# A narrow projection as four 32-column fp32 blocks side by side, and history transposes moved into the head, in a hybrid SSD and pooling decoder step

## The chip, the core and the metric

The kernel runs on one core of one Trainium2 chip. The metric is the device time of one execution in microseconds. Engines are named as in the profile: PE is TensorE's matrix work and PEld its weight loads, DVE is VectorE, ACT is ScalarE, POOL is GpSimd, SP is the engine that issues most DMAs.

## The reference

`x` is 1024 prompt tokens and 64 sample tokens (8 sequences of 8) of width 1024, in fp32. The part that the change touches:

```
h    = rmsnorm(x) * norm_pre                       # 1088 tokens x 1024
proj = h @ w_in                                    # split into z | xBC (1536) | dt (16) | u | g | gates (2048)
xBC  = silu(causal_conv4(concat(state_conv, xBC))) # sample rows start from 3 history rows per sequence
dt   = softplus(proj_dt + dt_bias)                 # 16 columns, one for each head
y    = ssd_scan(xBC, dt, -exp(a_log))              # everything of branch A waits for dt
```

Behind it come the gate by z and the grouped norm, a pooling branch, the two branch projections, the sigmoid merge, the output projection with a norm, and the states.

## The kernel before

Activations are held transposed, with model channels on the 128 partitions: `h` is split into two tiles `Hhi` and `Hlo` (128 x 8 blocks of channels x 1088 tokens) whose sum is the fp32 value; both are stored in a reduced form (fp32r) that PE streams in one pass. A projection takes three products for each of the 8 channel blocks (hi by hi, lo by hi, hi by lo), in three chunks of tokens (384, 384, 320), so a chunk is a group of 24 matmuls into one bank (`psum_main`, two banks with the tag `m0`). Weights come by DMA in slabs of 128 columns and are split the same way: ACT casts `whi`, then POOL or DVE subtracts for `wlo` (`split`, L94 and L95).

The order of everything is written out by hand. The list `main` holds PE's groups, one for each slot; `at(slot, fn, key)` puts work of the other engines behind a slot's group, sorted by key, and `at_pe` puts PE work ahead of it. Each engine then works its own list strictly in that order. The slots that matter here:

- slots 0 to 5: two conv tiles (`cv[0]`, `cv[1]`), chunk by chunk; slots 6 to 8: the three chunks of `cv[8]`; slot 9: the dt projection (`DtStep.group`); then `cv[10]` and so on.
- For a conv group of slot t, ACT copies the bank out in slot t+1 (`evac`, L335) and makes the first tap (L343), DVE does three taps in slot t+2 (`taps`, L349), and in slot t+3 ACT takes a tanh (L356) of their result and DVE combines it (`fin`, L357, L360).
- The head, before slot 0 and in the first slots, is the string `plan`: N is a squared sum of a tile of 128 tokens, S and D scale it (DVE, L210), T and U transpose its two halves (PE, L224), E and F split them into `Hhi` and `Hlo`, W splits a weight slab, H is a filler matmul of the identity by itself (L1156) whose result nobody reads.
- The dt step: `load` brings the 16 columns, `conv` splits them into 32 of 128 columns of `dsw` (hi beside lo, the rest zero), `group` runs 16 matmuls for each chunk, `evac` copies 32 rows, `tok` (L416) transposes them to tokens, `softplus` adds the two partial sums and goes on.
- `hist_T` transposes the 24 rows of conv history at slot 5 (L291), twice six transposes, and DVE copies them out.

Of the kernel before, what the change touches and what calls it, by code (L numbers as in the profile page):

```python
# [38 lines left out]
def hybrid_decoder_step(  # L39
# [47 lines left out]
    def bank(tag):  # L87
        return px.tile([128, 512], F32, tag=tag, name=nm(tag))
# [16 lines left out]
    def at_pe(slot, fn, *args, first=False):  # L105
        pe[slot].insert(0 if first else len(pe[slot]), (fn, args))
# [161 lines left out]
        nc.sync.dma_start(prow[68:72], pool_scale[0].rearrange("(t p) -> t p", p=128))  # L268

    def hist_dma():  # L270
        for hf in range(2):
            hr = pbox["h", hf] = s1.tile([24, 768], F32, tag="xn", bufs=4, name=nm("xn"))
            nc.sync.dma_start(hr, state_conv[0].rearrange("b k c -> (b k) c")[:, 768 * hf:768 * hf + 768])
        for q in range(2):
            nc.sync.dma_start(dsk[64 * q:64 * q + 64],
                              d_skip[0].rearrange("(j q) -> q j", q=2)[q].partition_broadcast(64),
                              allow_slow_non_contiguous=True)
        nc.sync.dma_start(bias_b, dt_bias[0].partition_broadcast(128))
        nc.sync.dma_start(na, a_log[0].partition_broadcast(128))

    def params_T():
# [2 lines left out]
        nc.vector.tensor_scalar(par[:, 0:60], ps[:, 0:60], 0.5, None, op0=ALU.mult)  # L284
        nc.vector.tensor_copy(par[:, 60:72], ps[:, 60:72])

    def hist_T():
        for hf in range(2):
            ps = bank("pst")
            for i in range(6):  # L290
                nc.tensor.transpose(ps[:, 24 * i:24 * i + 24], pbox["h", hf][:, 128 * i:128 * i + 128], ident[0:24, 0:24])  # L291
            nc.vector.tensor_copy(histc[hf], ps[:, 0:144].rearrange("p (i k) -> p i k", i=6))
        nc.scalar.activation(na, na, AF.Exp)
        nc.vector.tensor_scalar(na, na, -1.0, None, op0=ALU.mult)

# [73 lines left out]

    class DtStep:  # L370
        def load(self):
            self.raw = s1.tile([128, 8, 16], F32, tag="dst", name="dst")
            nc.sync.dma_start(self.raw, w_in[0].rearrange("(k p) e -> p k e", p=128)[:, :, C_DT:C_DT + 16])
            self.w = s1.tile([128, 8, 128], F32R, tag="dsw", name="dsw")
            nc.gpsimd.memset(self.w.bitcast(F32), 0.0)

        def conv(self):
            split(self.w[:, :, 0:16], self.w[:, :, 16:32], self.raw, nc.gpsimd)

        def group(self):  # L380
            box = {}

            def emit():
                for c, (a, b) in enumerate(CHUNKS):
                    ps = box[c] = bank(("m0", "pyo", "pyo")[c])
                    for k in range(8):
                        for p, h in enumerate((Hhi, Hlo)):
                            nc.tensor.matmul(ps[:, 0:b - a], self.w[:, k], h[:, k, a:b], start=k == 0 and p == 0,  # L388
                                             stop=k == 7 and p == 1)

            main.append(emit)
            t = len(main) - 1
# [12 lines left out]
        def evac(self, box):  # L405
            self.dtr = zt((32, LT))
            self.tmp = zt((128, 5, 9, 16))
            nc.gpsimd.memset(self.tmp[64:128, 0, 8], 0.0)
            for c, (a, b) in enumerate(CHUNKS):
                nc.scalar.copy(self.dtr[:, a:b], box[c][0:32, 0:b - a])  # L410

        def tok(self):
            self.pd = bank("pst")
            for t in range(9):
                n = 128 if t < 8 else NS
                nc.tensor.transpose(self.pd[0:n, 32 * t:32 * t + 32], self.dtr[:, 128 * t:128 * t + n], ident[0:32, 0:32])  # L416
            zfree(self.dtr)

        def softplus(self):
            v, tt, u, e, r = (self.tmp[:, i] for i in range(5))  # L420
            self.adt = v
            for n, t0, m in ((128, 0, 8), (NS, 8, 1)):
                d = v[0:n, t0:t0 + m]
                nc.vector.tensor_reduce(d, self.pd[0:n, 32 * t0:32 * t0 + 32 * m].rearrange("p (t i h) -> p t h i", t=m, i=2),
                                        axis=mybir.AxisListType.X, op=ALU.add)
# [722 lines left out]
    nrow = hst[0:1].rearrange("p u x -> p (u x)")  # L1148
    nc.sync.dma_start(nrow, norm_pre)
    loads = {"W": lambda i: cv[i].slab.dma(raw1[:, 0:1024].rearrange("p (k e) -> p k e", k=8) if i else None),  # L1150
             "X": load_x, "Q": lambda i: params_dma()}
    for w in "X0 X1 X2 X3 W0 Q0 X4 W1 X5 X6 X7 X8".split():
        loads[w[0]](int(w[1]))

    def H(i):
# [2 lines left out]
    def R(e):  # L1158
# [351 lines left out]
```

## Time and profile before

| | |
|---|---|
| median of 3 runs | 894.23 us (893.12 to 894.34) |
| the profiled execution | 894.35 us, span 892.6 us |
| PE busy | 879.9 us of the span (99%) |
| DVE, ACT, POOL busy | 62%, 39%, 24% |
| mean granted TensorE clock | 0.997 of 2.4 GHz |

PE is busy nearly all the time, so what moves the time is what lengthens or shortens PE's own list and what makes PE wait. A row of the chronological view has a start, a length, engine, line, operation, output and inputs, shapes, the count of merged instructions and, in brackets, how long the engine stood idle before and what ended that. Lengths of successive matmuls overlap; the distance between two starts is what one costs.

### The profile page before, as it was taken

The page shows a single profiled execution, that of the slowest core. Times are in us where ns is not written, and L with a number is a line of the kernel's source. Part 1 is how long each engine was busy: PE and PEld are TensorE (multiplying, and loading weights), DVE is VectorE, ACT ScalarE, POOL GpSimd, SP SyncE. Part 2 cuts the span into 40 slices and gives each one's busy share as a digit, 9 for nine tenths or more (in the row PEclk, how much of TensorE's full clock was granted, in tenths as well). Part 3 has the DMA queues.
Part 4 walks back from the last instruction along what each step waited for, and adds up shares of the span by engine and source line. Part 5 has one row for each costly group of instructions (what it writes and reads, how often), then busy time and mean ns, then how long its engine had stood idle before and what let it go on. Part 6 is the DMA issues. An engine that isn't in the chain of part 4 may idle for free.

```text
span 892.6 us, 14398 instructions
## 1 busy us (share of the span) xinstructions
PE 879.9 (99%) x5558; PEld 843.7 (95%) x5558; DVE 551.2 (62%) x999; ACT 348.8 (39%) x770; POOL 217.4 (24%) x297
## 2 busy tenths in 40 slices
PE   7999999999999999999999999999999999999997
PEld 5999999999999999999999999999999999988886
DVE  6776796989667765457746554357356627963322
ACT  6645565656375543345333141112333224331111
POOL 6332264756465652121100000000000000001101
PEclk9999999999999999999999999999999999999999
DMA  8010233342345335453311124433111123722322
GB/s 275 9 48 24 77 95 97 99 128 71 103 129 156 105 96 164 127 160 101 95 49 36 54 84 149 143 114 99 34 49 51 31 79 115 264 74 71 100 99 85
DMA packets 110322, 87.97 MB, mean 99 GB/s; under 512 B 8474, under 2 KB 97550, under 8 KB 110253
## 3 DMA queue, kind: packets, MB, share of 16 engines
q1 hardware_dynamic: 110109, 86.98, 32.5%
q8 instruction: 44, 0.72, 0.3%
q14 instruction: 25, 0.20, 0.1%
q10 hardware_dynamic: 144, 0.07, 0.0%
HBM read 69.46 MB, written 17.56 MB: 97 GB/s over the span
## 4 chain that ended last, share of the span: by engine, by line
PE 93%; DVE 1%; ACT 1%; POOL 1%; issue 0%; DVEq 0%; POOLq 0%; ACTq 0%
PE m L143 54%; PE pyo L143 16%; PE m L1399 3%; PE pyo L1399 3%; PE xb L1399 2%; PE pst L1399 2%; PE pyo L575 2%; PE pyo L582 2%; PE pst L586 1%; PE xb L711 1%; PE xb L542 1%; PE pyo L388 1%; DVE r L841 1%; PE pyo L752 1%; PE pst L759 0%
## 5 line engine op out<-in xcount | busy, mean ns | idle before, releaser
L143 PE MATMUL m<-Hhi,whi 128*128 128x384 f32 (+3 forms) x872 | 289.0, 331 | 0.0
L143 PE MATMUL m<-Hhi,wlo 128*128 128x384 f32 (+3 forms) x872 | 285.4, 327 | 0.0
L143 PE MATMUL m<-Hlo,whi 128*128 128x384 f32 (+3 forms) x872 | 285.3, 327 | 0.0
L143 PEld LDWEIGHTS m<-Hhi,whi 128*128 128x128 f32 x872 | 164.6, 189 | 0.6
L143 PEld LDWEIGHTS m<-Hlo,whi 128*128 128x128 f32 x872 | 164.6, 189 | 0.3
L143 PEld LDWEIGHTS m<-Hhi,wlo 128*128 128x128 f32 x872 | 164.4, 189 | 0.3
L349 DVE SCALAR_TENSOR_TENSOR r<-r,par,r 128x384 f32<-128x384 f32 (+3 forms) x108 | 94.6, 876 | 2.6
L94 ACT CAST whi<-raw 128x1024 fp32r<-128x1024 f32 (+1 forms) x67 | 59.8, 892 | 91.4 <-PE m L143 53.6
L95 DVE TENSOR_TENSOR wlo<-raw,whi 128x512 fp32r<-128x512 f32 (+1 forms) x46 | 43.4, 944 | 65.2 <-ACT whi L94 65.1
L95 POOL TENSOR_TENSOR wlo<-raw,whi 128x1024 fp32r<-128x1024 f32 x21 | 51.6, 2457 | 40.9 <-ACT whi L94 40.9
L143 PE MATMUL pyo<-Hhi,whi 128*128 128x384 f32 (+1 forms) x184 | 59.8, 325 | 0.0
L143 PE MATMUL pyo<-Hhi,wlo 128*128 128x384 f32 (+1 forms) x184 | 59.7, 325 | 0.0
L143 PE MATMUL pyo<-Hlo,whi 128*128 128x384 f32 (+1 forms) x184 | 59.7, 324 | 0.0
L143 PE MATMUL m<-z,whi 128*128 128x384 f32 (+1 forms) x217 | 54.0, 327 | 0.0
L143 PE MATMUL pyo<-z,whi 128*128 128x384 f32 (+1 forms) x191 | 47.7, 327 | 0.0
L568 POOL TENSOR_TENSOR sa<-sa,cb 128x512 f32<-128x512 f32 x28 | 39.8, 1441 | 3.7 <-ACT sa L564 3.7
L143 PEld LDWEIGHTS m<-z,whi 128*128 128x128 f32 x217 | 38.4, 188 | 0.0
L143 PE MATMUL m<-z,wlo 128*128 128x384 f32 (+1 forms) x115 | 37.6, 327 | 0.0
L563 ACT ACTIVATE sa<-sa,acm 128x128 f32<-128x128 f32 x112 | 35.6, 389 | 0.0
L609 DVE SCALAR_TENSOR_TENSOR z<-z,dsk,se 128x128 f32<-128x128 f32 x56 | 34.8, 660 | 1.0
L1434 POOL TENSOR_SCALAR t<-t 128x1 f32<-128x1 f32 (+1 forms) x9 | 2.5, 276 | 133.7 <-ACT q L1431 133.7
L143 PEld LDWEIGHTS pyo<-Hlo,whi 128*128 128x128 f32 x184 | 34.6, 188 | 0.0
(386 smaller groups left out, 1608.5 us busy)
## 6 DMA issues: line engine op xcount, KB each, us to landing
raw<-in_w_in_dram SPq DMA_DIRECT2D x43, 512.0 KB, 4.0
z<-in_x_prompt_dram SPq DMA_DIRECT2D x15, 512.0 KB, 4.5
sa<-dscr SPq DMA_DIRECT2D x28, 256.0 KB, 4.4
z<-spill SPq DMA_DIRECT2D x11, 544.0 KB, 5.1
raw<-in_w_branch_a_dram SPq DMA_DIRECT2D x16, 256.0 KB, 2.8
r<-in_w_out_dram SPq DMA_DIRECT2D x16, 256.0 KB, 4.4
se<-dscr SPq DMA_DIRECT2D x56, 64.0 KB, 3.8
out_dram<-q SPq DMA_DIRECT2D x14, 256.0 KB, 2.1
```

Of the source, the lines that this page charges most:

```text
L94: nc.scalar.copy(hi, src)
L95: (eng or nc.vector).tensor_tensor(lo, src, hi.bitcast(F32), op=ALU.subtract)
L143: nc.tensor.matmul(ps[:, 0:b - a], slab.w(k, p), rhs(k, p)[:, a:b], start=k == 0 and p == 0, stop=k == slab.kn - 1 and p == 2)
L349: nc.vector.scalar_tensor_tensor(A, R[:, k:k + w], cw(k, i), A, op0=ALU.mult, op1=ALU.add)
L388: nc.tensor.matmul(ps[:, 0:b - a], self.w[:, k], h[:, k, a:b], start=k == 0 and p == 0, stop=k == 7 and p == 1)
L542: nc.tensor.transpose(p[:, 128 * i:128 * i + 128], X[2 * self.u + i][:, self.cols], ident)
L563: nc.scalar.activation(A[:, h], A[:, h], AF.Relu, bias=acm[:, self.c, hh:hh + 1], scale=-1.0)
L568: nc.gpsimd.tensor_tensor(A, A, CBs[self.c, self.g].unsqueeze(1).to_broadcast([128, 4, 128]), op=ALU.mult)
L575: nc.tensor.matmul(py[64 * q:64 * q + 64, 128 * i:128 * i + 128], s.x0[:, 2 * i + q], s.A[:, 2 * i + q], start=True, stop=True)
L582: nc.tensor.matmul(py[:, 256 + 128 * i:384 + 128 * i], hs[:, 128 * i:128 * i + 128], Ct[self.g][:, self.cols], start=True, stop=True)
L609: nc.vector.scalar_tensor_tensor(xv, xv, dsk[:, j:j + 1], self.E[:, i] if self.c else py[:, 128 * i:128 * i + 128], op0=ALU.mult, op1=ALU.add)
L1399: nc.tensor.matmul(box["ps"][:, 0:b - a], lh, rh[k][:, a:b], start=kk == 0 and i == 0, stop=kk == 7 and rh is Wlo)
```

## The change

The dt weights stay whole fp32, in 32 columns of which 16 are filled (the rest zero); nothing is split. DVE makes eight fp32 tiles `h[k] = Hhi[k] + Hlo[k]` (`whole`, 128 x 1088 each), two behind each of slots 5 to 8. In slot 9 each chunk takes 8 fp32 matmuls of 32 output columns: four of them go to the four 32-column parts of the array and to four 32-partition parts of the bank, each with another channel block, and a second round of four adds to them. The four partial sums are transposed along (full 128 x 128 transposes, now in two `xb` banks and one `pst` bank) and added up in DVE's reduce.

The 24 history rows are loaded in three pieces early in SP's list, ahead of x tile 4; their twelve transposes (`I0`) stand in the head, in one `m0` bank, and ACT copies them out (`J0`) instead of DVE. Six more fillers H stand in the head.

```diff
     def hist_dma():
-        for hf in range(2):
-            hr = pbox["h", hf] = s1.tile([24, 768], F32, tag="xn", bufs=4, name=nm("xn"))
-            nc.sync.dma_start(hr, state_conv[0].rearrange("b k c -> (b k) c")[:, 768 * hf:768 * hf + 768])
...
+    def hist_load():
+        for i in range(3):
+            pbox["h", i] = rt(512)[0:24]
+            nc.sync.dma_start(pbox["h", i], state_conv[0].rearrange("b k c -> (b k) c")[:, 512 * i:512 * i + 512])
+
     def hist_T():
+        ps = pbox["hp"] = bank("m0")
+        for i in range(12):
+            nc.tensor.transpose(ps[:, 24 * i:24 * i + 24], pbox["h", i // 4][:, 128 * (i % 4):128 * (i % 4) + 128], ident[0:24, 0:24])
+
+    def hist_copy():
         for hf in range(2):
-            ps = bank("pst")
-            for i in range(6):
-                nc.tensor.transpose(ps[:, 24 * i:24 * i + 24], pbox["h", hf][:, 128 * i:128 * i + 128], ident[0:24, 0:24])
-            nc.vector.tensor_copy(histc[hf], ps[:, 0:144].rearrange("p (i k) -> p i k", i=6))
+            nc.scalar.copy(histc[hf], pbox["hp"][:, 144 * hf:144 * hf + 144].rearrange("p (i k) -> p i k", i=6))
...
     class DtStep:
         def load(self):
-            self.raw = s1.tile([128, 8, 16], F32, tag="dst", name="dst")
-            nc.sync.dma_start(self.raw, w_in[0].rearrange("(k p) e -> p k e", p=128)[:, :, C_DT:C_DT + 16])
-            self.w = s1.tile([128, 8, 128], F32R, tag="dsw", name="dsw")
-            nc.gpsimd.memset(self.w.bitcast(F32), 0.0)
-
-        def conv(self):
-            split(self.w[:, :, 0:16], self.w[:, :, 16:32], self.raw, nc.gpsimd)
+            self.w = s1.tile([128, 8, 32], F32, tag="dsw", name="dsw")
+            nc.gpsimd.memset(self.w, 0.0)
+            nc.sync.dma_start(self.w[:, :, 0:16], w_in[0].rearrange("(k p) e -> p k e", p=128)[:, :, C_DT:C_DT + 16])
+
+        def whole(self, k):
+            if k == 0:
+                self.h = []
+            self.h.append(zt())
+            nc.vector.tensor_tensor(self.h[k], Hhi[:, k].bitcast(F32), Hlo[:, k].bitcast(F32), op=ALU.add)
...
                 for c, (a, b) in enumerate(CHUNKS):
                     ps = box[c] = bank(("m0", "pyo", "pyo")[c])
-                    for k in range(8):
-                        for p, h in enumerate((Hhi, Hlo)):
-                            nc.tensor.matmul(ps[:, 0:b - a], self.w[:, k], h[:, k, a:b], start=k == 0 and p == 0,
-                                             stop=k == 7 and p == 1)
+                    for r in range(2):
+                        for g in range(4):
+                            k = 4 * r + g
+                            nc.tensor.matmul(ps[32 * g:32 * g + 32, 0:b - a], self.w[:, k], self.h[k][:, a:b], start=r == 0,
+                                             stop=r == 1, tile_position=(0, 32 * g))
+                zfree(*self.h)
...
-    for w in "X0 X1 X2 X3 W0 Q0 X4 W1 X5 X6 X7 X8".split():
+    for w in "X0 X1 X2 X3 W0 Q0 Y0 X4 W1 X5 X6 X7 X8".split():
...
-    plan = ("R0 N0 R1 H0 N1 D0 H0 T0 U0 S1 N2 H0 S2 T1 N3 U2 T2 F0 W0 S3 E0 U1 E1 H0 T3 H0 U3 N4 F1 D4 W1 | "
+    plan = ("R0 N0 R1 H0 N1 D0 H0 T0 U0 S1 N2 H0 S2 T1 N3 H0 H0 U2 T2 F0 W0 S3 E0 U1 E1 I0 H0 H0 H0 H0 T3 J0 H0 U3 N4 F1 D4 W1 | "
...
-    at_pe(5, hist_T)
+    at(4, na_T, key=9)
...
-    at(6, dts.conv, key=5)
+    for k in range(8):
+        at(5 + k // 2, dts.whole, k, key=9)
```

On DVE, the stretch that ends with slot 9 stood so before (r are the conv's work tiles, z its outputs; L349 are the taps, L357 and L360 the combinations with the tanh):

```order
L357 SCALAR_TENSOR_TENSOR z_349<-r_694,r_607 128x384
L360 SCALAR_TENSOR_TENSOR z_349<-r_694,r_607 128x64
L349 SCALAR_TENSOR_TENSOR r_647<-r_640,par,r_647 128x472 x3
L357 SCALAR_TENSOR_TENSOR z_390<-r_731,r_647 128x384
L360 SCALAR_TENSOR_TENSOR z_390<-r_731,r_647 128x64
L349 SCALAR_TENSOR_TENSOR r_692<-r_689,par,r_692 128x384 x3
L357 SCALAR_TENSOR_TENSOR z_688<-r_798,r_692 128x384
L349 SCALAR_TENSOR_TENSOR r_729<-r_726,par,r_729 128x384 x3
```

and stands so in the changed kernel, where L363 and L366 are the combinations, L355 the taps and L386 the new sums:

```order
L363 SCALAR_TENSOR_TENSOR z_380<-r_710,r_617 128x384
L366 SCALAR_TENSOR_TENSOR z_380<-r_710,r_617 128x64
L355 SCALAR_TENSOR_TENSOR r_661<-r_654,par,r_661 128x472 x3
L386 TENSOR_TENSOR z_717<-Hhi,Hlo 128x1088
L386 TENSOR_TENSOR z_719<-Hhi,Hlo 128x1088
L363 SCALAR_TENSOR_TENSOR z_421<-r_751,r_661 128x384
L366 SCALAR_TENSOR_TENSOR z_421<-r_751,r_661 128x64
L355 SCALAR_TENSOR_TENSOR r_708<-r_705,par,r_708 128x384 x3
L386 TENSOR_TENSOR z_758<-Hhi,Hlo 128x1088
L386 TENSOR_TENSOR z_760<-Hhi,Hlo 128x1088
L363 SCALAR_TENSOR_TENSOR z_704<-r_798,r_708 128x384
L355 SCALAR_TENSOR_TENSOR r_749<-r_746,par,r_749 128x384 x3
```

The last pair of sums (channel blocks 6 and 7) stands behind the taps of slot 8, which are those of `cv[8]`'s first chunk; two pairs like these stand earlier, behind the taps of slots 5 and 6.

On ACT in the head, before (xn are normalised token tiles, raw and z_120 weight slabs; L201 is the squared sum of x tile 4, L94 the casts):

```order
L94 CAST Hhi<-pyo_192 128x4x128
L201 ACTIVATE xn_245,t_243<-z_137 128x1024
L94 CAST Hhi<-pyo_222 128x4x128
L94 CAST whi_253<-z_120 128x1024
L94 CAST Hhi<-pst_208 128x4x128
```

and in the changed kernel:

```order
L94 CAST Hhi<-pyo_198 128x4x128
L296 COPY histc_107<-m_47_239 128x144
L296 COPY histc_108<-m_47_239 128x144
L201 ACTIVATE xn_276,t_274<-z_143 128x1024
L94 CAST Hhi<-pyo_232 128x4x128
L94 CAST whi_284<-z_120 128x1024
L94 CAST Hhi<-pst_218 128x4x128
```

The two history copies stand ahead of the squared sum of x tile 4 and of the cast of the second weight slab, and wait for PE's history transposes. PE's list in the same place, changed kernel (L1169 are fillers, L224 the transposes T and U, L292 those of the history):

```order
L224 MATMUL pst_213<-ident,xn_191 128x128 x4
L224 MATMUL pst_218<-ident,xn_191 128x128 x4
L224 MATMUL pyo_232<-ident,xn_170 128x128 x4
L292 MATMUL m_47_239<-ident,r_137 128x24 x4
L292 MATMUL m_47_239<-ident,r_139 128x24 x4
L292 MATMUL m_47_239<-ident,r_141 128x24 x4
L1169 MATMUL m_48_252<-ident 128x128
L1169 MATMUL m_49_254<-ident 128x128
L1169 MATMUL m_50_256<-ident 128x128
L1169 MATMUL m_51_258<-ident 128x128
L224 MATMUL xb_260<-ident,xn_205 128x128 x4
```

Between the transposes of tile 1 (`pyo_232`) and of tile 3 (`xb_260`) stood one filler before; now the twelve history transposes and four fillers stand there, the third of which (`m_50`) takes the history's bank and so waits for ACT's copies.

## Rows read from the trace of the kernel before

**Rows 1.** The page: busy us, share of the span and count for each engine, and the shares by engine of the chain that ended last.

```profile
PE 879.9 (99%) x5558; PEld 843.7 (95%) x5558; DVE 551.2 (62%) x999; ACT 348.8 (39%) x770; POOL 217.4 (24%) x297
PE 93%; DVE 1%; ACT 1%; POOL 1%; issue 0%; DVEq 0%; POOLq 0%; ACTq 0%
```

**Rows 2.** Busy time by stretch: the stretch's ends and length, then busy us of PE, PEld, DVE, ACT and POOL with counts, granted clock, share of DMA, GB/s.

```profile
13.00:16.00 3.00, 0.89 (x9) 0.70 (x6) 3.00 (x1) 2.62 (x5) 2.92 (x2) 1.00 1.01 395
17.30:20.60 3.30, 3.30 (x18) 3.30 (x16) 3.30 (x5) 1.80 (x4) 3.13 (x3) 0.50 0.94 202
```

**Rows 3.** PE in order of time around the dt projection (L388): its first matmul, its last and the next group's first.

```profile
60.88 0.34 PE L388 MATMUL m<-Hhi,dsw 128*128 128x384 f32 x1
...
68.74 0.31 PE L388 MATMUL pyo<-Hlo,dsw 128*128 128x320 f32 x1
68.89 0.34 PE L143 MATMUL m<-Hhi,whi 128*128 128x384 f32 x1
```

**Rows 4.** PE in order of time where the kernel already runs eight fp32 matmuls of 32 output columns, 128 tokens wide, in the four column parts (L752; each leaves two records), the group ahead and the work behind.

```profile
359.54 0.33 PE L143 MATMUL m<-Hlo,whi 128*128 128x384 f32 x1
359.71 0.34 PE L143 MATMUL m<-Hhi,wlo 128*128 128x384 f32 x1
359.98 0.64 PE L752 MATMUL pyo<-hT,hst 128*32 128x128 f32 x16
360.56 0.73 PE L759 MATMUL pst<-bk,z 96*128 96x512 f32 x2
361.13 1.04 PE L711 MATMUL xb<-ident,h 128*128 128x128 f32 x8
361.92 0.42 PE L143 MATMUL m<-Hhi,whi 128*128 128x384 f32 x1
```

**Rows 5.** DVE in order of time from slot 5's combination to the one behind the dt projection.

```profile
48.16 0.56 DVE L357 SCALAR_TENSOR_TENSOR z<-r,r 128x384 f32<-128x384 f32 x1 [1.49 <-ACT r L356]
...
51.15 0.56 DVE L357 SCALAR_TENSOR_TENSOR z<-r,r 128x384 f32<-128x384 f32 x1 [0.59 <-ACT r L356]
51.62 4.28 DVE L349 SCALAR_TENSOR_TENSOR r<-r,par,r 128x472 f32<-128x472 f32 x3
56.70 0.56 DVE L357 SCALAR_TENSOR_TENSOR z<-r,r 128x384 f32<-128x384 f32 x1 [0.80 <-ACT r L356]
57.18 0.22 DVE L360 SCALAR_TENSOR_TENSOR z<-r,r 128x64 f32<-128x64 f32 x1
57.31 2.19 DVE L349 SCALAR_TENSOR_TENSOR r<-r,par,r 128x472 f32<-128x472 f32 x3
60.17 0.56 DVE L357 SCALAR_TENSOR_TENSOR z<-r,r 128x384 f32<-128x384 f32 x1 [0.67 <-ACT r L356]
...
60.79 1.92 DVE L349 SCALAR_TENSOR_TENSOR r<-r,par,r 128x384 f32<-128x384 f32 x3
...
69.96 0.56 DVE L357 SCALAR_TENSOR_TENSOR z<-r,r 128x384 f32<-128x384 f32 x1 [4.27 <-ACT r L356]
```

**Rows 6.** DVE operations that read two fp32 operands from SBUF, grouped by line and shape: count, busy us, mean ns of one, idle before.

```profile
L95 DVE TENSOR_TENSOR wlo<-raw,whi 128x1024 fp32r<-128x1024 f32 x22 | 26.9, 1223 | 41.7 <-ACT whi L94 41.7
L841 DVE TENSOR_TENSOR r<-r,r 128x384 f32<-128x384 f32 x12 | 6.7, 558 | 1.4 <-ACT r L840 0.3
```

**Rows 7.** POOL in order of time: the split of a weight slab beside the long taps of rows 5.

```profile
52.13 2.44 POOL L95 TENSOR_TENSOR wlo<-raw,whi 128x1024 fp32r<-128x1024 f32 x1 [2.05 <-ACT whi L94]
```

**Rows 8.** PE in order of time at the history transposes (L291) and at dt's transposes (L416), each with the group behind.

```profile
43.21 0.91 PE L291 MATMUL pst<-ident,xn 24*128 24x24 f32 x12
44.05 0.47 PE L143 MATMUL m<-Hhi,whi 128*128 128x448 f32 x1
...
77.31 0.71 PE L416 MATMUL pst<-ident,z 32*128 32x32 f32 x9
77.95 0.42 PE L143 MATMUL m<-Hhi,whi 128*128 128x320 f32 x1
```

**Rows 9.** PE in order of time in the head.

```profile
16.32 0.63 PE L224 MATMUL xb<-ident,xn 128*128 128x128 f32 x4 [2.43 <-DVE xn L210]
...
19.53 0.41 PE L143 MATMUL m<-Hhi,whi 128*128 128x256 f32 x1
19.74 0.41 PE L143 MATMUL m<-Hlo,whi 128*128 128x256 f32 x1
...
21.11 0.28 PE L143 MATMUL m<-Hhi,whi 128*128 128x256 f32 x1
21.23 0.28 PE L143 MATMUL m<-Hlo,whi 128*128 128x256 f32 x1
...
22.34 0.60 PE L224 MATMUL pyo<-ident,xn 128*128 128x128 f32 x4
```

**Rows 10.** The other engines in the head, in order of time: ACT's squared sum of x tile 4 and cast of the second slab, POOL's split of that slab, DVE's scaling of tile 4 (in two halves) and the subtraction behind it.

```profile
12.45 1.07 ACT L201 ACTIVATE xn<-z 128x1024 f32<-128x1024 f32 x1
...
14.18 1.05 ACT L94 CAST whi<-z 128x1024 fp32r<-128x1024 f32 x1
...
16.82 2.38 POOL L95 TENSOR_TENSOR wlo<-z,whi 128x1024 fp32r<-128x1024 f32 x1
17.89 2.53 DVE L210 SCALAR_TENSOR_TENSOR xn<-z,t,z 128x512 f32<-128x512 f32 x2
20.34 0.68 DVE L95 TENSOR_TENSOR Hlo<-pst,Hhi 128x512 fp32r<-128x512 f32 x1
```

More of the change, by code (lines that the diff above doesn't have):

```diff
@@ L285, in params_T, with na_T @@
         nc.vector.tensor_copy(par[:, 60:72], ps[:, 60:72])
+    def hist_load():
+        for i in range(3):
+            pbox["h", i] = rt(512)[0:24]
+            nc.sync.dma_start(pbox["h", i], state_conv[0].rearrange("b k c -> (b k) c")[:, 512 * i:512 * i + 512])
     def hist_T():
+        ps = pbox["hp"] = bank("m0")
+        for i in range(12):
+            nc.tensor.transpose(ps[:, 24 * i:24 * i + 24], pbox["h", i // 4][:, 128 * (i % 4):128 * (i % 4) + 128], ident[0:24, 0:24])
+    def hist_copy():
         for hf in range(2):
-            ps = bank("pst")
-            for i in range(6):
-                nc.tensor.transpose(ps[:, 24 * i:24 * i + 24], pbox["h", hf][:, 128 * i:128 * i + 128], ident[0:24, 0:24])
-            nc.vector.tensor_copy(histc[hf], ps[:, 0:144].rearrange("p (i k) -> p i k", i=6))
+            nc.scalar.copy(histc[hf], pbox["hp"][:, 144 * hf:144 * hf + 144].rearrange("p (i k) -> p i k", i=6))
+    def na_T():
         nc.scalar.activation(na, na, AF.Exp)
@@ L405, in evac @@
         def evac(self, box):
-            self.dtr = zt((32, LT))
+            self.dtr = zt()
             self.tmp = zt((128, 5, 9, 16))
@@ L409, in evac @@
             for c, (a, b) in enumerate(CHUNKS):
-                nc.scalar.copy(self.dtr[:, a:b], box[c][0:32, 0:b - a])
+                nc.scalar.copy(self.dtr[:, a:b], box[c][:, 0:b - a])
         def tok(self):
-            self.pd = bank("pst")
+            self.pd = [bank("xb"), bank("xb"), bank("pst")]
             for t in range(9):
                 n = 128 if t < 8 else NS
-                nc.tensor.transpose(self.pd[0:n, 32 * t:32 * t + 32], self.dtr[:, 128 * t:128 * t + n], ident[0:32, 0:32])
+                q = 128 * (t % 4)
+                nc.tensor.transpose(self.pd[t // 4][0:n, q:q + 128], self.dtr[:, 128 * t:128 * t + n], ident)
             zfree(self.dtr)
@@ L421, in softplus @@
             self.adt = v
+            for n, t0, m in ((128, 0, 4), (128, 4, 4), (NS, 8, 1)):
+                d = v[0:n, t0:t0 + m]
+                nc.vector.tensor_reduce(d, self.pd[t0 // 4][0:n, 0:128 * m].rearrange("p (t g x) -> p t x g", t=m, g=4)[:, :, 0:16],
+                                        axis=mybir.AxisListType.X, op=ALU.add)
             for n, t0, m in ((128, 0, 8), (NS, 8, 1)):
                 d = v[0:n, t0:t0 + m]
-                nc.vector.tensor_reduce(d, self.pd[0:n, 32 * t0:32 * t0 + 32 * m].rearrange("p (t i h) -> p t h i", t=m, i=2),
-                                        axis=mybir.AxisListType.X, op=ALU.add)
                 nc.vector.tensor_tensor(d, d, bias_b[0:n].unsqueeze(1).to_broadcast([n, m, 16]), op=ALU.add)
@@ L1150, in hybrid_decoder_step @@
     loads = {"W": lambda i: cv[i].slab.dma(raw1[:, 0:1024].rearrange("p (k e) -> p k e", k=8) if i else None),
-             "X": load_x, "Q": lambda i: params_dma()}
-    for w in "X0 X1 X2 X3 W0 Q0 X4 W1 X5 X6 X7 X8".split():
+             "X": load_x, "Q": lambda i: params_dma(), "Y": lambda i: hist_load()}
+    for w in "X0 X1 X2 X3 W0 Q0 Y0 X4 W1 X5 X6 X7 X8".split():
         loads[w[0]](int(w[1]))
@@ L1163, in hybrid_decoder_step @@
     steps.update({"H": H, "R": R, "W": lambda i: cv[i].slab.conv(nc.gpsimd), "V": lambda i: cv[i].slab.conv(nc.vector),
-                  "P": lambda i: params_T(), "K": lambda i: consts()})
-    plan = ("R0 N0 R1 H0 N1 D0 H0 T0 U0 S1 N2 H0 S2 T1 N3 U2 T2 F0 W0 S3 E0 U1 E1 H0 T3 H0 U3 N4 F1 D4 W1 | "
+                  "I": lambda i: hist_T(), "J": lambda i: hist_copy(), "P": lambda i: params_T(), "K": lambda i: consts()})
+    plan = ("R0 N0 R1 H0 N1 D0 H0 T0 U0 S1 N2 H0 S2 T1 N3 H0 H0 U2 T2 F0 W0 S3 E0 U1 E1 I0 H0 H0 H0 H0 T3 J0 H0 U3 N4 F1 D4 W1 | "
             "T4 E2 E3 F2 N5 E4 N6 S5 P0 S6 F3 U4 F4 | "
```

## The prediction

> **What bounds the kernel now.** The page first: PE is busy 99% of the span and makes 93% of the chain that ended last, DVE is busy 62% [rows 1]. So time is won only by shortening PE's list or by taking away PE's few waits, and lost wherever PE is made to wait. An average of 62% says nothing of DVE in one stretch, though, and the change puts new DVE work into one stretch, just ahead of PE work that needs it; so the second view is DVE in order of time there. From the combination of slot 5 to the end of slot 8's taps, 48.16 to 60.79 + 1.92 = 62.71, DVE stands idle for only 0.59 + 0.80 + 0.67 = 2.06 of 14.55 us [rows 5]. PE starts the dt projection at 60.88 [rows 3], 1.8 us before those taps end. Today that harms nobody: dt needs nothing of DVE. The third view is PE around the edits themselves: dt, the history, the head.
>
> **dt on PE alone.** Before, dt lasts from 60.88 to the next group's start at 68.89: 8.01 us [rows 3]. The new form has no fp32 matmul of 384 columns in the trace to go by, but the kernel already runs eight fp32 matmuls in the four column parts, 128 wide: 0.58 us from their first start to the next work's [rows 4]. If eight of these shared nothing, each with two records of two passes, at the plain pass's 0.173 for 384 columns (359.54 to 359.71), that is 0.058 for 128, they would take 32 x 0.058 = 1.85 us. Four side by side give 0.46, which leaves 0.12 for starting and draining. So I take a round of four records at two passes, 0.346 us for 384 columns; four rounds make a chunk, 1.38; at 0.15 a pass [rows 3] the chunk of 320 costs 1.20. PE's own need is 1.38 + 1.38 + 1.20 + 0.12 = 4.1 us, 3.9 less than before. Bounds: if all of 0.58 scales with the width, 1.74 + 1.74 + 1.45 = 4.9; if the records were one pass each and 0.35 of it fixed, 2.3.
>
> The Trainium skill (TensorE: Matmul & The Clock Gate, Part 3, packing small matmuls) gives three column parts 2.38 times, not 3 times. Taken over to four parts as an estimate, 3.17 times, dt would cost PE some 5.1 us. The sum below keeps the row's value, and the page's would make it 0.7 longer.
>
> **The eight sums on DVE decide it.** Each adds two fp32 operands from SBUF over 1088 columns. DVE's nearest row has 1024 columns and takes 1.223 us; the all-fp32 one with 384 takes 0.558, so the type brings no faster pace [rows 6]. 1088 columns are 1.30, and since successive starts on DVE overlap by 0.08 (56.70 + 0.56 against 57.18, rows after one another) [rows 5], one costs 1.22 and eight 9.8 us. DVE's list is strict, and the last two sums stand behind slot 8's taps. Their end follows from the stretch above: 62.71, less the three waits for ACT's tanh (the 2.06) that now are filled with sums, plus 9.8, is 70.4. POOL's split of a slab, 52.13 for 2.44 us [rows 7], nearly stops the DVE taps beside it: they take 4.28 where the next such three take 2.19 [rows 5]. In the new order it meets a sum instead, which reads two SBUF operands too, so that loss stays and is in the 14.55 already. If DVE could overlap none of the tanh waits, the end is 2 us later. If the whole stretch starts earlier by the head's gain (0.3, below), it ends at 70.1.
>
> The history's removal from slot 5 doesn't help here: it shortens PE behind the group that frees the first slab, and this stretch of DVE is started by ACT and POOL work on that group.
>
> So PE comes to slot 9 at 60.88 - 0.94 - 0.3 = 59.6, does what the early sums allow, and stands. Behind the last sum PE has: this block's two records, 0.69, two chunks, 1.38 + 1.20, and 0.12: 3.4 us (1.9 to 4.1 by the bounds above). dt ends at 73.5 instead of 68.89: **+4.6**. The 3.9 that dt gets shorter and PE's gains ahead of slot 9 are all waited away. What stands behind dt on DVE is no later than this: today DVE idles 4.27 us before 69.96 for a tanh that waits behind ACT's copies of dt [rows 5], and that pattern moves along.
>
> **The clock.** Between 59.6 and 70.1 PE has some 2.7 us of work. In the head it stood 2.43 us before 16.32 and then ran at a granted clock of 0.50 from 17.30 to 20.60, with starts 0.21 apart (19.53, 19.74) where the same matmuls later stand 0.12 apart (21.11, 21.23) [rows 2, 9]. That stretch cost 3.3 x (1 - 0.12/0.21) = 1.4 us; the fp32 passes have nothing else to wait for and should take twice as long, 1.65. I take **+1.6**; bounds 0 (the clock stays up) and 3.3 (two such stretches). The Trainium skill (the same page, Part 1) calls the slow clock the default that activity lifts; by that rule the term is sure, and the head's row agrees.
>
> **The rest.** dt's transposes were nine of 32 columns, 77.31 to 77.95, 0.64 us [rows 8]; now nine full ones: eight such take 361.13 to 361.92, 0.79 [rows 4], so 0.89: **+0.25** (0.1 to 0.4). ACT's three copies of 128 partitions in place of 32 have the same columns. The split of the weights leaves ACT and POOL, hidden before and after.
>
> The history's twelve transposes leave PE's list: 43.21 to 44.05 and some 0.1 ahead, 0.94 us [rows 8], which ends in the wait at dt. In the head they and four fillers stand in PE's wait of 2.43 us, 13.89 to 16.32 [rows 9]; the twelve and four fillers of some 0.2 make 1.8, so they cost PE nothing, even with a short wait for ACT's copies among them. If the clock stays up there, the first group is over by up to 1.4 us earlier. But ACT's history copies stand ahead of its squared sum of tile 4, which began at 12.45 [rows 10]: ACT now waits for PE's history, until 13.89 + 0.94 = 14.8 at the latest, and all behind it, the cast of the second slab among it, comes some 2.4 us later (an estimate): at 16.6, not 14.18. POOL's split then starts near 17.7, not 16.82, and lies over the whole of DVE's scaling of tile 4 from 17.89 [rows 10]. This scaling and the subtraction behind it, which ended at 21.0, end near 22.0. The parameters' transpose waits for the bank of that subtraction, and with it the transposes at 22.34 [rows 9]. So I take 0.3 us for the head (0 to 1.4).
>
> **Sum.** 4.6 + 1.6 + 0.25 = 6.45 us on the profiled execution's 894.35 gives **900.8 us**; the median of the runs shown, 894.23, is 0.1 below it. Nothing behind dt absorbs a delay: PE is busy throughout.
>
> **Rivals.** A difference of 0.2%, 1.8 us, is about what a measurement of this kernel can tell from none.
>
> - The clock doesn't fall at dt: 899.2. For it: PE does some work with each pair of sums. Against it: the head. 0.18, inside the same mechanism; with the slow clock 0.66.
> - Faster: the sums are ready when dt starts. Then dt saves 3.9, the history 0.94, the head 0.3, less 0.25: 889.5. It decides at the end of the last sum: if it comes before about 65.3 (68.89 - 3.4 - 0.25), the kernel is no slower. It takes sums at 0.6 us each, twice the pace of every row of this kind, or a stretch that starts 5 us earlier. For it speaks only DVE's 62%. 0.10.
> - About even: sums half as late as I reckon, because part of the stretch moves up with the head and ACT, and no slow clock: 893 to 896. 0.06.
> - The four parts don't run side by side: the chunks after the last sum cost four times as much, 10.3 in place of 2.6, so 908. Rows 4 speak against it. 0.02 inside slower.
>
> Slower in all is 0.84, faster 0.10, the same 0.06. The range goes from 897.4 (the clock stays up, the head gives 1.0, the passes run at their lower bound) to 903.6 (the slow clock twice as long and another 1 us of DVE beside POOL); it leaves out the faster case and the even one. The likeliest alone: 899.8 to 902.6.
>
> **What would show it.** In the changed kernel's trace: PE waits for DVE's sums by name at the dt matmuls, longest for the last pairs, 8 us and more in all; the last sum ends near 70; each lasts 1.3, one of them near 3 beside POOL's split; the granted clock is 0.50 in a stretch behind that; from the last sum to the next group 3.4 us at full clock, near 5 at half; the dt matmuls come in fours within hundredths of a microsecond. I am wrong if no wait for DVE stands in slot 9, if the sums take half of 1.3, or if the clock stays up where PE stands.

## The result and the profile after

The changed kernel takes 899.92 us (899.62 to 900.82, 6 runs) where the kernel before takes 893.69 (893.09 to 894.45, 6 runs beside them): 1.007 times, interval 1.006 to 1.0081. It is slower, as forecast, by 6.2 us; the forecast was 900.8, and the range 897.4 to 903.6 holds the time. The profiled execution took 899.9.

The times of the kernel before fall on two levels, near 893.0 and 894.2, and the profiled execution of before (894.35) belongs to the upper one; an experiment below looks at what the upper level pays for.

The page of the changed kernel, busy us and the chain by engine, answers to [rows 1]; DVE now has 4% of the chain, where it had 1%:

```profile
PE 882.5 (98%) x5568; PEld 839.0 (93%) x5568; DVE 561.3 (62%) x1006; ACT 349.1 (39%) x771; POOL 216.2 (24%) x296
PE 91%; DVE 4%; issue 2%; ACT 1%; POOL 1%; DMA 1%; DVEq 0%; SPq 0%; POOLq 0%; ACTq 0%
```

DVE in order of time, the counterpart of [rows 5] (L363 is the combination, L386 the sums, two to a row), and then POOL's split of a slab, the counterpart of [rows 7]:

```profile
47.35 0.56 DVE L363 SCALAR_TENSOR_TENSOR z<-r,r 128x384 f32<-128x384 f32 x1 [1.51 <-ACT r L362]
...
49.67 2.48 DVE L386 TENSOR_TENSOR z<-Hhi,Hlo 128x1088 f32<-128x1088 f32 x2
52.07 2.75 DVE L363 SCALAR_TENSOR_TENSOR z<-r,r 128x384 f32<-128x384 f32 x1
...
56.85 2.49 DVE L386 TENSOR_TENSOR z<-Hhi,Hlo 128x1088 f32<-128x1088 f32 x2
...
61.97 2.49 DVE L386 TENSOR_TENSOR z<-Hhi,Hlo 128x1088 f32<-128x1088 f32 x2
...
66.82 2.49 DVE L386 TENSOR_TENSOR z<-Hhi,Hlo 128x1088 f32<-128x1088 f32 x2
...
75.08 0.56 DVE L363 SCALAR_TENSOR_TENSOR z<-r,r 128x384 f32<-128x384 f32 x1 [3.47 <-ACT r L362]
```

```profile
51.33 3.07 POOL L95 TENSOR_TENSOR wlo<-raw,whi 128x1024 fp32r<-128x1024 f32 x1 [2.04 <-ACT whi L94]
```

From 47.35 to the last sum's end, 66.82 + 2.49 = 69.31, no row has an idle time (nor have the rows left out here): DVE is full there. POOL's split began while a sum was under way and fell on the combination at 52.07, which took 2.75 in place of 0.56. The pair of sums ahead of it kept its 2.48, and the split took 3.07 in place of 2.44.

PE at dt (L397), against [rows 3], and PE's waits there in the table of waits (us in total, times, longest):

```profile
60.59 0.85 PE L397 MATMUL m<-z,dsw 128*32 128x384 f32 x8 [1.35 <-ACT r L341]
63.31 2.69 PE L397 MATMUL m<-z,dsw 128*32 128x384 f32 x4 [1.87 <-DVE z L386]
68.16 2.05 PE L397 MATMUL m<-z,dsw 128*32 128x384 f32 x3 [2.15 <-DVE z L386]
...
70.01 4.15 PE L397 MATMUL pyo<-z,dsw 128*32 128x384 f32 x29
74.09 0.44 PE L143 MATMUL m<-Hhi,whi 128*128 128x384 f32 x1
```

```profile
PE m L397 <- DVE z L386: 4.0, 2, 2.2
...
PE m L397 <- ACT r L341: 1.4, 1, 1.4
```

PE reaches slot 9 at 60.59 - 1.35 = 59.24, and the next group starts at 74.09, 4.78 us behind the last sum, where it was 68.89. So dt takes 14.85 us from PE's arrival. The table has only 4.0 us of waits for sums in it, because the ends of matmuls are modelled: the row at 63.31 holds two blocks, the second of which started only when its sum was done at 64.46, and the table counts nothing there. Busy time by stretch shows the clock (columns as in [rows 2]):

```profile
60.59:62.38 1.79, 0.85 (x8) 0.15 (x8) 1.74 (x3) 1.00 (x2) 0.02 (x1) 1.00 0.00 0
62.38:69.31 6.93, 3.84 (x6) 0.54 (x6) 6.86 (x10) 1.99 (x5) 1.32 (x5) 0.50 0.01 2
69.31:72.62 3.31, 3.31 (x25) 1.41 (x28) 2.23 (x4) 0.48 (x1) 0.00 (x0) 0.50 0.00 0
72.62:74.09 1.47, 1.47 (x18) 0.53 (x11) 0.00 (x0) 0.48 (x1) 0.00 (x0) 1.00 0.00 0
```

PE in the head, in place of [rows 9]: history, fillers, then the parameters' transpose, which now waits for DVE's subtraction, and the transposes that stood at 22.34:

```profile
13.61 0.92 PE L292 MATMUL m<-ident,r 24*128 24x24 f32 x12
14.46 1.58 PE L1169 MATMUL m<-ident 128*128 128x128 f32 x8
...
21.84 0.28 PE L280 MATMUL pst<-ident,m 72*128 72x72 f32 x1 [0.61 <-DVE Hlo L95]
21.96 0.60 PE L224 MATMUL pyo<-ident,xn 128*128 128x128 f32 x4
```

DVE's scaling of tile 4 and that subtraction, against [rows 10]:

```profile
17.88 3.30 DVE L210 SCALAR_TENSOR_TENSOR xn<-z,t,z 128x512 f32<-128x512 f32 x2
21.11 0.68 DVE L95 TENSOR_TENSOR Hlo<-pst,Hhi 128x512 fp32r<-128x512 f32 x1
```

### The profile page after: what moved, and what is told of

Its sections match the earlier page's. It is cut to its first block, busy times and chain, and to the rows that moved or that the text cites. A ratio compares the mean times of both kernels' runs of the same rounds, so it can differ in the third digit from the quotient of the medians.

```text
span 898.2 us, 14420 instructions
## 1 busy us (share of the span) xinstructions
PE 882.5 (98%) x5568; PEld 839.0 (93%) x5568; DVE 561.3 (62%) x1006; ACT 349.1 (39%) x771; POOL 216.2 (24%) x296
## 4 chain that ended last, share of the span: by engine, by line
PE 91%; DVE 4%; issue 2%; ACT 1%; POOL 1%; DMA 1%; DVEq 0%; SPq 0%; POOLq 0%; ACTq 0%
PE m L143 53%; PE pyo L143 16%; PE m L1413 3%; PE pyo L1413 3%; PE xb L1413 2%; PE pst L1413 2%; PE pyo L588 2%; PE pyo L595 2%; PE pst L599 1%; DVE z L386 1%; DVE r L355 1%; PE xb L724 1%; PE xb L555 1%; DVE r L854 1%; PE pyo L765 1%
## 5 line engine op out<-in xcount | busy, mean ns | idle before, releaser
L94 ACT CAST whi<-raw 128x1024 fp32r<-128x1024 f32 (+1 forms) x67 | 59.8, 892 | 91.3 <-PE m L143 53.5
L355 DVE SCALAR_TENSOR_TENSOR r<-r,par,r 128x384 f32<-128x384 f32 (+3 forms) x108 | 92.5, 856 | 2.6
```

The lines of the kernel that those rows point to most:

```text
L355: nc.vector.scalar_tensor_tensor(A, R[:, k:k + w], cw(k, i), A, op0=ALU.mult, op1=ALU.add)
```

## Experiments

**Theory:** the eight sums on DVE set the end of dt, and the clock falls while PE stands for them. **Rivals:** dt's new form costs PE itself; DVE has slack; the clock term isn't real; the head counts.

**The sums left out.**

```diff
-            nc.vector.tensor_tensor(self.h[k], Hhi[:, k].bitcast(F32), Hlo[:, k].bitcast(F32), op=ALU.add)
...
-    nc.tensor.matmul(..., self.w[:, k], self.h[k][:, a:b], ...)
+    nc.tensor.matmul(..., self.w[:, k], Hhi[:, k, a:b].bitcast(F32), ...)
```

> The changed kernel with the eight sums left out: PE multiplies the high half alone as fp32 (the low half's share of dt is left out), everything else stays. Theory: no wait for DVE at dt, PE's own need of 4.1 us is seen bare, dt ends near 63.4 and the clock stays up: 893.7 - 5.5 + 0.3 = 888.5. Rival 1 (the four parts share something, 5.1 us bare): 889.5. Rival 2 (it is not the sums but dt's new form on PE that costs): no faster than 897.

Measured: 888.94 us (888.83 to 889.19), before 893.08 beside it, ratio 0.9951 (0.9934 to 0.9967). PE at dt in order of time (here L394):

```profile
59.34 1.50 PE L394 MATMUL m<-Hhi,dsw 128*32 128x384 f32 x16
60.66 2.55 PE L394 MATMUL pyo<-Hhi,dsw 128*32 128x384 f32 x32
63.14 0.44 PE L143 MATMUL m<-Hhi,whi 128*128 128x384 f32 x1
```

Bare, dt is 63.14 - 59.34 = 3.80 us, a chunk of 384 columns 1.32. So dt's new form on PE does what it is meant to, and the whole loss of 11.0 us against this kernel is the sums', with the waits and the slow clock that they bring.

**The sums doubled.**

```diff
-            nc.vector.tensor_tensor(self.h[k], ...)
+            for _ in range(2):
+                nc.vector.tensor_tensor(self.h[k], ...)
```

> The changed kernel with each of the eight sums made twice, one after the other. Theory (DVE has no idle time in the stretch, the last sum sets dt's end): eight more sums of 1.22 move the last sum by 9.8, and the whole by as much: 909.7. Rival 1 (DVE has slack there): half of it or less, 905 or below. Rival 2 (PE's own side of dt decides): no change, 899.9.

Measured: 911.87 us (911.46 to 912.36), 12.0 above the changed kernel and 2.2 more than the theory had. DVE's last four sums (L387) in order of time, and then PE's next group behind dt:

```profile
75.04 5.14 DVE L387 TENSOR_TENSOR z<-Hhi,Hlo 128x1088 f32<-128x1088 f32 x4
```

```profile
85.84 0.45 PE L143 MATMUL m<-Hhi,whi 128*128 128x384 f32 x1
```

The last sum ends at 80.18, 10.9 later; a pair grew from 2.49 to 5.14, 1.32 for each added sum, not 1.22. From there to the next group it is 5.66 in place of 4.78: more of dt fell into the slow clock (granted 0.50 until 85.27). Both rivals fall: PE pays what DVE is given, in full.

**Fillers in PE's waits.**

```diff
+                pf = bank("pst")
+                for _ in range(7):
+                    nc.tensor.matmul(pf[:, 0:384], ones_r, Hhi[:, 0, 0:384], start=True, stop=True)
...
+                            for _ in range({(0, 4): 10, (0, 5): 4, (0, 6): 18, (0, 7): 4}.get((c, k), 0)):
+                                nc.tensor.matmul(pf[:, 0:384], ones_r, Hhi[:, 0, 0:384], start=True, stop=True)
```

> The changed kernel with 43 filler matmuls (one pass of 384 columns into a bank nobody reads) put in PE's waits around dt's first chunk, so that PE works through them; sums and dt unchanged. Theory (the clock falls because PE stands): the granted clock stays up, the 3.3 us at half behind the last sum shrink to 1.9, 1.4 us less than the changed kernel: 898.5. Rival (the clock term is something else, or the fillers delay dt): 899.9 or more.

Measured: 900.00 us (899.85 to 900.11), with a mean granted clock of 0.999 in place of 0.993. Taken alone it speaks for the rival, but the test was confounded: dt's last block started at 71.06 behind a sum that ended at 67.09 + 2.49 = 69.58, since there were too many fillers. So again, with `{(0, 4): 10, (0, 5): 2, (0, 6): 13, (0, 7): 1}`:

> As e_fill, with 33 fillers in place of 43, so few that PE is through with them when each sum comes (in e_fill dt's seventh block started 1.1 us behind its sum, its eighth 1.5 us behind). Theory: with the clock up and PE on time, the 4.78 us from the last sum to the next group become 3.1 to 3.4, so 1.4 to 1.7 us less than the changed kernel's 899.9: 898.4. Rival: 899.9, the clock term isn't real.

Measured: 898.50 us (898.34 to 898.65, 5 runs). Busy time in the stretch behind its last sum, and then PE's next group:

```profile
69.52:72.70 3.18, 3.18 (x35) 1.26 (x35) 2.23 (x4) 0.96 (x2) 0.00 (x0) 1.00 0.00 0
```

```profile
72.70 0.44 PE L143 MATMUL m<-Hhi,whi 128*128 128x384 f32 x1
```

The same work takes 3.18 at 1.00 and 4.78 with most of it at 0.50 (1.2 GHz): the clock costs 1.4 us of time, 1.6 in these rows.

**Dt's part alone, the head's part alone.** In the one, `hist_dma`, `hist_T`, the loads and the plan are those of before; in the other, `DtStep` and its places in the schedule are.

> Only dt's part: eight sums on DVE and the four column parts; head and history as before. Theory: the end of dt follows from DVE's stretch, which starts 0.8 us later than in the changed kernel (48.16 instead of 47.35), so 0.8 us slower than the changed kernel, 900.7, whatever PE's list lost ahead of it. Rival (gains add up): slower by what e_head gains, 1.3, so 901.2. In both PE waits for the sums and the clock falls behind them.

> Only the head's part of the change: the history's load, transposes and copies moved, the six fillers; the dt projection as before. Theory (sums on DVE decide at dt): here nothing waits behind, so the 0.94 us of history transposes and the 0.38 us of the head count in full: 1.3 us less than before, 892.4. Rival (what leaves PE's list is waited away again at the next bank or tanh, also without the sums): 0 to -0.4, 893.5.

Measured: dt's part 899.95 us (899.82 to 900.90, 4 runs), at its median the same as the whole change; the head's part 892.63 us (892.51 to 892.80, 10 runs) against 893.08 (892.90 to 894.25) of before, ratio 0.999 (0.9981 to 1.0). The 900.7 expected of dt's part fits one of its four executions, the profiled one (900.9): there DVE's stretch begins at 48.07 and the last sum ends at 70.04, 0.73 later than in the changed kernel. The other three took 899.8 to 900.1, and no profile of those was taken. The head's part by itself is worth 0.4 us against the lower level of before and 1.6 against the upper one, and the interval just reaches no gain at all. Beside the sums the medians show no gain from it: what PE saves ahead of slot 9 it waits away.

**What the head is worth, and the two levels.** The kernel before once more, and the head's part without its six fillers:

```diff
-    plan = ("... N3 H0 H0 U2 T2 F0 W0 S3 E0 U1 E1 I0 H0 H0 H0 H0 T3 J0 H0 U3 N4 F1 D4 W1 | "
+    plan = ("... N3 U2 T2 F0 W0 S3 E0 U1 E1 I0 T3 J0 H0 U3 N4 F1 D4 W1 | "
```

> The kernel before, unchanged, for another profiled execution. Theory: where the time is near 893.0 the granted clock doesn't fall in the head, and PE's transposes at 22.34 come earlier by the 1.2 us between the two levels; near 894.2 it falls as in the profile shown.

> Only the head's part of the change, without its six fillers: the history's load, transposes and copies in the head, dt as before. Question: what keeps the head's clock up. The times of before fall on two levels, 893.0 and 894.2; the profiled one (894.35) has the granted clock at half from 17.3 to 20.7; e_head has one level, 892.6. Theory (the fillers are needed): two levels again, some 1.2 apart, the lower near 892.6. Rival (the history's twelve transposes are enough): one level, 892.6.

Measured: 892.92 us, with the granted clock at 1.00 where [rows 2] have 0.50. Of this execution of before, one after the other: busy time of the stretch, the subtraction on DVE, PE's transposes behind it:

```profile
17.30:20.60 3.30, 3.30 (x30) 3.27 (x28) 3.30 (x4) 1.69 (x4) 3.13 (x3) 1.00 1.08 177
```

```profile
20.25 0.68 DVE L95 TENSOR_TENSOR Hlo<-pst,Hhi 128x512 fp32r<-128x512 f32 x1
```

```profile
21.10 0.60 PE L224 MATMUL pyo<-ident,xn 128*128 128x128 f32 x4
```

These transposes stand at 21.10; in the profile of before with the fall they stand at 22.34, and in the changed kernel at 21.96. The fall costs 1.24 us, which is the distance of the two levels. But the upper level needs no fall. The profiled execution of dt's part (900.9), whose head is that of before, has none on record in its head. Its first projection nevertheless starts slowly, with matmuls 0.21 us apart until 19.34 and 0.12 apart from 19.55, and the transposes stand at 22.33 all the same:

```profile
18.91 0.41 PE L143 MATMUL m<-Hhi,wlo 128*128 128x256 f32 x1
19.13 0.41 PE L143 MATMUL m<-Hhi,whi 128*128 128x256 f32 x1
...
19.67 0.28 PE L143 MATMUL m<-Hhi,whi 128*128 128x256 f32 x1
19.79 0.28 PE L143 MATMUL m<-Hlo,whi 128*128 128x256 f32 x1
...
22.33 0.60 PE L224 MATMUL pyo<-ident,xn 128*128 128x128 f32 x4
```

So a fall in the head and a late rise cost the same 1.2 us. Which of the two the other executions of the upper level had isn't known.

The changed kernel's profile has no fall in the head, but DVE's subtraction stands 0.86 later (21.11 in place of 20.25, behind POOL's split, which now lies over the scaling). At these transposes it is 0.38 ahead of the upper level and 0.86 behind the lower one; further on the history's 0.94 leaves PE's list.

Of the ten fillers in the changed kernel's head the variant leaves four; the kernel before has five (so the change adds five, not six, and one of the six taken out here stood in the kernel before). Without the six the ten times lie between 892.58 and 893.96, with them between 892.51 and 892.80: the fillers remove the slower executions. The clock in those isn't seen, since the profiled execution is the fastest of the ten; and they spread (893.34 and 893.52 among them) rather than fall on one upper level.

**The sums one slot earlier.**

```diff
-        at(5 + k // 2, dts.whole, k, key=9)
+        at(4 + k // 2, dts.whole, k, key=9)
```

> The changed kernel with the pairs of sums behind the taps of slots 4 to 7 in place of 5 to 8; dt stays in slot 9. Theory: the last sum loses the combination and taps that stood ahead of it, 2.4 us, and up to 1.5 us of the idle time at 46 to 47.3; it ends near 65.4 to 66.9, dt 3.4 to 4.8 behind it, so 2.4 to 4 us less than the changed kernel: 896.7. Rival (the sums delay the conv's taps and banks instead, and PE stands there): 899.9 or more.

Measured: 895.22 us (894.51 to 895.91, 10 runs), ratio to before 1.002 (1.0011 to 1.0029). PE's waits and the group behind dt:

```profile
56.51 0.42 PE L143 MATMUL m<-Hhi,whi 128*128 128x320 f32 x1 [0.85 <-ACT r L341]
...
61.65 1.49 PE L397 MATMUL m<-z,dsw 128*32 128x384 f32 x12 [1.36 <-ACT r L341]
...
68.70 0.44 PE L143 MATMUL m<-Hhi,whi 128*128 128x384 f32 x1
```

The last sum ended at 65.52, the next group follows 3.18 later at full clock: in this execution the clock did not fall at dt, and that is where it beats the theory. PE still waits 1.6 us for sums, and a new wait for ACT's copy (L341) stands in slot 8, 0.85. The ten times fall on two levels, five at 894.5 to 894.8 and five at 895.7 to 895.9, with the median between them. Only one of the lower level was profiled (894.53), so what the upper one pays for stays open.

**Dt three slots later.**

```diff
             cv[i].group(c)
-        if i == 8:
-            dts.group()
+            if (i, c) == (10, 2):
+                dts.group()
...
-            at_pe(t + 3, self.tok)
+            at_pe(t + 2, self.tok)
```

What follows `tok` moves one slot nearer in the same way, and the opening of the scan's tile pools (`open_s`) from slot 9 to 12. (The sample rows of the scan read their decay factors before they are written here, since three steps placed relative to dt moved with it; the amount of work is the same.)

> The changed kernel with dt's group three slots later, behind the chunks of the next conv tile (its transposes and sums one slot closer to it, its store just ahead of the first load that needs it). Theory: PE comes to dt near 71.9, after the last sum at 69.3, waits for nothing, and dt costs its bare 3.8: as with no sums, 888.9, 4.1 us less than before (to 890 if the closer steps behind dt make a wait of their own). Rival (dt's lateness is paid in the scan, which waits for it): 893 or more.

Measured: 898.61 us (898.33 to 898.71, 5 runs). PE in order of time:

```profile
72.83 0.42 PE L143 MATMUL m<-Hhi,whi 128*128 128x320 f32 x1 [2.40 <-ACT r L341]
...
76.55 1.50 PE L397 MATMUL m<-z,dsw 128*32 128x384 f32 x16
...
80.34 0.44 PE L143 MATMUL m<-Hhi,whi 128*128 128x384 f32 x1
```

The theory falls. Dt itself costs its bare 3.79 and waits for nothing, but PE now stands for the conv's banks: 2.40 here, 1.36 and 0.67 in the slots ahead. ACT's copies out of the banks wait for DVE (in the changed kernel 2.48 us, the row below), and DVE is late by the sums wherever dt stands. Further waits follow behind dt, the largest 1.2; not all of the 9.7 us above the kernel without sums is accounted for.

```profile
60.05 0.48 ACT L341 COPY r<-m 128x384 f32<-128x384 f32 x1 [2.48 <-DVE z L366]
```

**One sum for each slot from 4 to 11**, dt three slots later, the three steps back on their old slots:

```diff
-        at(5 + k // 2, dts.whole, k, key=9)
+        at(4 + k, dts.whole, k, key=9)
```

> The changed kernel with one sum behind each of the slots 4 to 11 in place of two behind 5 to 8, and dt's group three slots later, behind the chunks of the next conv tile, with what follows it on its old slots or one nearer. Theory (it is DVE's load in the stretch that PE pays, not dt's place alone: with dt three slots later and the sums in pairs PE still stood 4.5 us for banks that wait for DVE's taps): one sum for a slot fits into the wait for the tanh (0.6) and the 1.2 by which DVE's step is shorter than PE's, so PE stands nowhere and dt costs 3.8: 889.0 to 890. Rival (what DVE is given there, PE waits for, wherever it stands): 893 or more.

Measured: 898.19 us (896.78 to 898.62, 5 runs), ratio 1.0049 (1.0036 to 1.0062). Two of the five took 896.8 and 897.0, three 898.2 to 898.6; the rows are of the fastest. DVE's last sum, and then PE's longest wait at dt, for that sum:

```profile
76.79 1.28 DVE L386 TENSOR_TENSOR z<-Hhi,Hlo 128x1088 f32<-128x1088 f32 x1
```

```profile
78.13 0.85 PE L397 MATMUL m<-z,dsw 128*32 128x384 f32 x1 [2.68 <-DVE z L386]
```

Missed again, for another reason: the conv's banks are in time (one wait of 1.0), but DVE works a slot's list some 5 us after PE has left the slot. The sum of slot 11 is done at 78.07, where PE came to slot 12 at 72.27 - 1.01 = 71.3. I had counted slots as if the engines stood in the same one.

**Four sums in place of eight**, early; the other four channel blocks are multiplied by the high and the low half:

```diff
-                    for r in range(2):
-                        for g in range(4):
-                            k = 4 * r + g
-                            nc.tensor.matmul(ps[32 * g:32 * g + 32, 0:b - a], self.w[:, k], self.h[k][:, a:b], start=r == 0, ...
+                    blocks = [(k, h[:, k].bitcast(F32)) for k in range(4, 8) for h in (Hhi, Hlo)] + list(enumerate(self.h))
+                    for i, (k, h) in enumerate(blocks):
+                        g = i % 4
+                        nc.tensor.matmul(ps[32 * g:32 * g + 32, 0:b - a], self.w[:, k], h[:, a:b], start=i < 4, ...
...
-    for k in range(8):
-        at(5 + k // 2, dts.whole, k, key=9)
+    for k in range(4):
+        at((4, 4, 5, 6)[k], dts.whole, k, key=9)
```

> The changed kernel with four sums in place of eight, behind the taps of slots 4, 4, 5 and 6 (two of them where DVE stood idle ahead of 47.6); channel blocks 4 to 7 are multiplied twice instead, by the high and by the low half, so that a chunk has three rounds of four column parts, the summed blocks last. The result is the same sum. Theory (DVE's load sets the loss, PE's need is 3.8 for two rounds): dt costs PE 5.7 bare, the last sum ends near 59 to 60, ahead of its round at 60.6, PE waits for nothing: the head's part alone is 892.6, less 8.0 - 5.7 = 2.3, plus 0.3 for the transposes: 890.6. Rival (half of the sums already push the conv's banks and dt): 892.6 or more.

Measured: 891.98 us (891.67 to 892.17, 11 runs), before 894.19 (892.96 to 894.54) beside it, ratio 0.9979 (0.997 to 0.9988); against before's lower level, 893.0, it is 1.0 us faster. DVE's last sum, and then PE at dt:

```profile
57.88 1.29 DVE L386 TENSOR_TENSOR z<-Hhi,Hlo 128x1088 f32<-128x1088 f32 x1
```

```profile
60.41 0.51 PE L397 MATMUL m<-Hhi,dsw 128*32 128x384 f32 x1 [1.23 <-ACT r L341]
...
66.03 0.44 PE L143 MATMUL m<-Hhi,whi 128*128 128x384 f32 x1
```

Dt takes 5.62 (5.7 expected) and no sum is waited for; nearly all of the 1.4 us by which it missed 890.6 is the wait of 1.23 for ACT's copy, the conv chain's share of the four sums. It beats both kernels. Its sums are fewer and stand earlier, and no run takes the two apart.

## Why the prediction was right, point by point

- **The sums decide dt's end: right.** PE waits for them by name at dt. Left out they give back 11.0 us, doubled they cost 12.0. Each lasts 1.25 in a pair, against the 1.22 to 1.30 reckoned from [rows 6]. Of the signs named ahead, 8 us of waits for sums did not appear as such: the table of waits has 4.0. What PE lost is in the distances instead, 14.85 us for dt from arrival to end against 3.80 bare.
- **When the last sum ends: 69.31, not 70.1.** The stretch began at 47.35, 0.5 earlier than the 48.16 - 0.3 I took (the head, below), and the rest lasted 0.3 less. This is nearly all of the 0.9 us by which the forecast was too high.
- **POOL's split meets a sum: wrong in place, right in price.** No sum was slowed, and none lasted near 3 us. The combination at 52.07, which reads two SBUF operands as well, took 2.75 in place of 0.56: 2.2 us lost, where the taps had lost 2.1.
- **Dt on PE alone, 4.1: measured 3.80.** A round is 1.32 / 4 = 0.33, not 0.346. The scaling of [rows 4] held, inside its bounds of 2.3 and 4.9. The Trainium skill's 2.38 times for three column parts (TensorE: Matmul & The Clock Gate, Part 3) would by my estimate have made it 5.1. Here four parts of 32 columns share nothing that shows (in the run with 33 fillers the two records of a block alone start 0.35 us apart, and so do those of four blocks side by side), and the measurement decides.
- **The wait I had not seen:** 1.35 at the start of dt for ACT's copy of a conv bank. It cost nothing here, since the sums came later still; where the sums come in time it is what is left to pay (1.23 with four sums).
- **The clock, +1.6: measured 1.4,** by the fillers that keep it at full (1.6 in the rows). Granted 0.50 (1.2 GHz) from 62.38 to 72.62, in which PE was busy for 3.84 of the first 6.93 us.
- **Dt's end: +5.20** (74.09 against 68.89), where the sum had 4.6 + 1.6 = 6.2. With the transposes, 0.26 more as forecast (0.25), 894.35 + 5.46 = 899.8, and the profiled execution took 899.9: nothing behind dt gave anything back.

```profile
82.52 1.04 PE L427 MATMUL xb<-ident,z 128*128 128x128 f32 x8
...
83.42 0.39 PE L143 MATMUL m<-Hhi,whi 128*128 128x320 f32 x1
```

- **The head, 0.3: mis-sized.** At the transposes that I reckoned with it is 0.38, by the mechanism I gave (the subtraction ends at 21.79, 22.0 forecast). But at the group that stood at 38.05 and now stands at 37.31 it is 0.74: in the kernel before PE stands 0.33 us there for DVE's scaling of the last tile, and the changed kernel does not. The extra 0.44 fits the 0.4 to 0.5 us by which DVE's stretch and PE's arrival at slot 9 came earlier than forecast. The rows are of before, and then of the changed kernel:

```profile
36.69 0.46 PE L224 MATMUL pst<-ident,xn 64*128 64x64 f32 x4 [0.33 <-DVE xn L210]
...
38.05 0.47 PE L143 MATMUL m<-Hhi,whi 128*128 128x448 f32 x1
```

```profile
37.31 0.47 PE L143 MATMUL m<-Hhi,whi 128*128 128x448 f32 x1
```

- **The execution that the forecast starts from** is one of the upper level. About half of the executions of before (35 of the 64 timed beside these runs) lie on the lower one. The execution profiled on that level (892.92) has the group of the last row at 36.72, and against it the head's edits lose 0.59 by there. I took one profiled execution for the kernel; two levels 1.2 us apart in its times, 893.12 beside 894.23 and 894.34, stood in the table. This choice did not make the forecast right or wrong: the same 6.45 us on 892.92 give 899.4, inside the range too.
- **The range:** by the three terms that I named its lower end comes to 897.0, not 897.4. Nothing hangs on it here.
- **The history's 0.94 is waited away: right.** With and without the head's part the kernel takes 899.9 at its median.

## What to carry to other kernels

Taking 4 us off the bound engine by giving 10 us to one that is 62% busy is a loss if the work stands in a stretch where that engine has only 2 us idle: look at the helper in order of time between the point where its input exists and the point where its result is needed. When an engine works its list in order, moved work delays everything behind it, so a later deadline for the moved work won 1.3 to 1.7 us of the 11.0 and no more. An earlier start won 4.7, and half of the work, placed where DVE stood idle, won 7.9 and was the only variant with sums that beat the kernel before. And a forecast against one profiled execution should first ask on which level of the kernel's times that execution lies.

## What the runs showed of the hardware

- Four fp32 matmuls of 32 output columns in the four column parts run at the pace of one: a round of four records over 384 columns takes 0.33 us, and the records of one block alone start 0.35 apart. One full-width fp32r pass over 384 columns costs 0.173 ([rows 4]).
- The granted clock fell to 0.50 at 62.38, after PE had stood for 1.35 us, worked for 0.85 and stood again for a sum. It was full again at 72.62; PE had worked without a gap since 69.31. With 33 fillers in the waits it did not fall.
- DVE operations with two SBUF operands stood nearly still beside POOL's two-operand split: the taps before (4.28 for 2.19), the combination after (2.75 for 0.56). A sum that was under way when the split began kept its pace, and then the split took 3.07 in place of 2.44.
- The kernel before has two times 1.2 us apart on the same input. In the profiled execution of the upper one the clock falls in the head; in that of dt's part, with the same head, PE's pace rose late at the same cost. Six small fillers in the changed head removed the slower times.
